# The pool projection as seven products in the mix, and the time step moved into the first gate block

## The chip, the cores and the metric

One core of a Trainium2 chip runs the whole program. The metric is device time in microseconds (us), the median of repeated runs. The engines of the core are named as in the profile: PE multiplies matrices, with PEld loading its stationary operand; DVE works on vectors; ACT evaluates activations and copies; POOL is the general engine, whose queue also issues DMAs; SP only issues DMAs. Each engine executes its own instructions in a fixed order and waits for others by semaphores. PE writes to PSUM, which has eight banks here; everything else is in SBUF or in memory.

## What is computed

One layer of a streaming encoder for 256 prompt tokens and 8 x 16 sample tokens together: T = 384 tokens, model width 2048, all in float32. The parts that matter here:

```
P = rmsnorm(x) @ w_in           # pool 2048 | z 4096 | x,B,C 6144 | dt 64 | two gates 4096
A = pool_mixer(pool part)       # windowed means minus self, a 512x512 map per group, a scale
B = ssd_scan(conv(x,B,C), dt) -> gated norm        # 4096 wide, state-space branch
m = sigmoid(g_A) * (A @ w_pool_proj) + sigmoid(g_B) * (B @ w_ssd_proj)
x = x + rmsnorm(m @ w_out)
x = x + rmsnorm(relu(rmsnorm(x) @ w_up)^2 @ w_down)
```

The change concerns `A @ w_pool_proj` (384 x 2048 by 2048 x 2048), where it is computed, and the small part `dt` (softplus, cumulative sums and their exponentials for 64 heads).

## The kernel before

**Products.** PE multiplies float32 as three products of a high and a low part: every operand x is split into h (a rounded copy, made on ACT) and l = x - h (made on DVE). A 128 x 1024 tile of a weight is one unit: SP loads it (`wfetch`), ACT and DVE split it (`wsplit`, lines 71 and 72, or `split`, 1166 and 1167) into tiles `wh` and `wl` of a ring of three each, and PE uses it in three matmuls per 128 rows of it. A tile of the ring is given out again when its last reader is done. The tile framework sorts the instructions of each engine once, at build time, mainly in program order and by what is ready; `behind(i)` and `later()` put instructions behind one, or behind the last weight split, on the same engine only.

**Direct projections.** `moving` multiplies the activations (stationary) by weight tiles (512 moving columns) for three blocks of 128 tokens: 18 matmuls for a unit, 8 units for an output block of 512 columns when the depth is 2048. `gate` does so for a gate block; after each unit it calls a hook, in which other work is traced. Line 155 to 157 are its three matmuls.

**Seven products.** `quad` multiplies by tile sums in the manner of Strassen and Winograd: a pair of token blocks, two halves of the depth and two halves of the output take 7 products instead of 8, and the third token block rides along with 4, so there are 11 products (of 2 x 3 matmuls, lines 1215 to 1217) for what is 12 directly. A quad covers 512 rows of the weight and 1024 columns of the output (`np_` is the half of the output). Its seven forms, in `ORDER`, each take one weight tile or one sum of weight tiles. Two tiles are added by a DMA of POOL's queue (line 1179), three sums are made on DVE (1202). The nine accumulators m per half are tiles of `acc`; those in `SEEDED` are copied by ACT into PSUM before the products and back after them (1187, 1192), the others are added on DVE (1194). `DIFFS` are five differences of activation tiles that the products need (line 1284, DVE), `refill` splits the activation tiles (ACT, DVE), `aload` fetches them from memory. `converted` turns the accumulators into the product, by seven additions.

**Order of the stages.** (1) The pool input is projected for 16 tiles, windowed and mapped per group; the first gate block `ga0` stands between (`gate_a`). At the end `dt_phase` computes the time step, then the last group is mapped; `pool_map` leaves the 16 pooled tiles in SBUF, split, as A. (2) `pool_out` multiplies A by `w_pp` directly, for four output blocks. The first is multiplied by its gate, the others are stored in memory. `dt_turn` turns the time step over by PE behind the first block. (3) Eight groups of the state-space branch, each with ten projections; at the end two gate blocks of the second gate (`gb0`, `gb1`). Each group stores its tiles in memory (`a_scr`). (4) The mix: the gate blocks `gb2`, `ga1`, `ga2`, `ga3` and part of `gb3` are multiplied unit by unit, and after each unit the hook traces a number of forms of `A_ssd @ w_ssd` (8 groups x 2 quads x 7 = 112 forms over 34 hooks). `gate_late` multiplies a gate by the stored pool product. (5) The merged m is turned over and multiplied by `w_out`. (6) The MLP, whose down projection also runs as quads between the units of the up projection.

Of the kernel before, what the change touches and what calls it, by code (L numbers as in the profile page):

```python
# [6 lines left out]
F32 = mybir.dt.float32  # L7
# [10 lines left out]
NB = 8  # L18
# [8 lines left out]
NWARM = 6  # L27

# [5 lines left out]
def build(ctx, tc, io):  # L34
# [180 lines left out]

    def newton(y, a, hm):
# [14 lines left out]
    def norm_bc(pool, sumsq, n, name, after=None, parts=None):  # L231
# [12 lines left out]
    pp_scr, ma_scr, gb_scr = (  # L244
        [[dram.tile([P, 512], F32, name=f"{nm}_scr{i}_{b}") for b in range(3)] for i in range(4)] for nm in ("pp", "ma", "gb")
    )
    t_scr = [dram.tile([T, P], F32, name=f"t_scr{i}") for i in range(40)]
# [155 lines left out]
    with tc.tile_pool(name="phc", bufs=1, reuse_waits="tile") as pc, tc.tile_pool(name="phc2", bufs=2, reuse_waits="tile") as pc2:  # L403
        pst = pc.tile([P, KD, NB, 15], F32, name="pst")
        gp.dma_start(pst, io["state_pool"])
        bufs = []
        for i in range(2):
# [3 lines left out]
        A = [  # L411
            (pc.tile([P, T], F32R, name=f"ah{n}"), pc.tile([P, T], F32R, name=f"al{n}")) for n in range(KD)
        ]
# [60 lines left out]
        def pool_map(gi, after=None):  # L474
            for hf in range(2):
                h, l = wload(io["pool_w"][gi, hf], f"pw{gi}_{hf}")
                for n2 in range(2):
                    n = gi * 4 + hf * 2 + n2
                    o = sstile(f"pw{n}")[:, :T]
                    with behind(after):  # L480
# [3 lines left out]
                    ah, al = (halves(a) for a in A[n])  # L484
                    sc = vec[:, V_PSC + n : V_PSC + n + 1]
                    s.activation(ah, even_odd(o), AF.Copy, scale=sc)
                    v.scalar_tensor_tensor(
                        out=al, in0=even_odd(o), scalar=sc, in1=ah.bitcast(F32), op0=ALU.mult, op1=ALU.subtract
                    )

        def gate_a(hook):
            sg = [pc.tile([P, 512], F32, tag=f"sg{b}", name=f"sg{b}") for b in range(3)]
            o = three("ga0")

            def done(b):
                with later():
                    sigmoid(sg[b], o, b)

            gate("w_ga", 0, o, done, hook)
            return sg  # L500

        def pool_out(nb, sg):
            o = three(f"pp{nb}")

            def done(b):
                if nb == 0:
                    v.tensor_tensor(sg[b], o[b], sg[b], ALU.mult)
                    gp.dma_start(ma_scr[0][b], sg[b])
                    return
                t = pc.tile([P, 512], F32, tag=f"sg{b}", name=f"po{nb}_{b}")  # L510
                s.copy(t, o[b])
                gp.dma_start(pp_scr[nb][b], t)

            moving(o, units_of("w_pp", nb), A, 1, done)

        def dt_phase(pb):
            ps = mmtile("pj_dt")[:, :T]
            for q in range(2):
# [6 lines left out]
                for k in range(8):  # L525
                    c = hl[:, k].rearrange("p a n -> p (a n)")
                    te.matmul(pairs(ps), c, woven(xg[q * 8 + k][0]), start=q + k == 0, stop=False)
                    te.matmul(pairs(ps), c, woven(xg[q * 8 + k][1]), start=False, stop=q * 8 + k == KD - 1)
# [10 lines left out]
            s.activation(e, ab, AF.Exp, scale=-1.0)  # L539
            v.tensor_scalar(t1, e, 2.0, None, ALU.add)  # L540
# [4 lines left out]
            for i in range(8, 0, -1):  # L545
                v.scalar_tensor_tensor(out=q, in0=q, scalar=1.0 / (2 * i + 1), in1=t2, op0=ALU.add, op1=ALU.mult)
            v.scalar_tensor_tensor(out=q, in0=q, scalar=1.0, in1=t1, op0=ALU.add, op1=ALU.mult)
# [6 lines left out]
            sy.dma_start(cum_scr, cum)  # L554
            nb = n64("nb")
# [21 lines left out]
        def dt_turn(srcs):  # L577
            for r in range(2):
                part = srcs[r * 8 : r * 8 + 8]
                o = sstile(f"tk{r}")  # L580
                for i, a in enumerate(part):
                    te.transpose(o[:, i * NH : i * NH + NH], a, ident[:NH, :NH])
# [10 lines left out]
        for gi in range(4):  # L593
            for k4 in range(4):
# [5 lines left out]
                if gi and k4 == (gi == 1):  # L600
                    if gi == 1:
                        count = []

                        def hook():
                            count.append(1)
                            if waiting and len(count) % 2 == 0:
                                with later():
                                    waiting.pop(0)()
# [1426 lines left out]
```

## Time and profile before

| | |
|---|---|
| median of three runs | 2581.05 us (2579.37 to 2581.16) |
| the profiled execution | 2581.39 us |
| its span, first to last instruction | 2579.6 us |
| pool stage, to the first product of the old pool projection | 0 to 200.3 us |
| old pool projection | 200.3 to 325.9 us |
| state-space groups and two gate blocks | 325.9 us to about 1092 |
| the mix | about 1092 to 1465 us |
| merge and output projection | about 1465 to 1605 us |
| MLP | about 1605 us to the end |

In the rows of the profile, a row of the timeline has start, length, engine, line, operation, the tiles that it writes and reads, shapes, and in brackets the idle time before it and what ended that. A row of a group ends in its busy time, the mean length of one in ns, and its idle time. A row of a stretch has the busy time and count of instructions of PE, PEld, DVE, ACT and POOL, then the granted clock, the DMA share and GB/s. A row of waits has who waited for whom: us in total, times, longest.

### The profile page before, as it was taken

Reading aid. Unit: us, or ns where it says so; the run is one execution under the profiler, and the core shown is the slowest. Engines: PE = TensorE matmul, PEld = TensorE weight load, DVE = VectorE, ACT = ScalarE, POOL = GpSimd, SP = SyncE. Lnnn points to the kernel's source line nnn. Section 1 sums busy time; section 2 is a strip of 40 time slices with the busy share of each in tenths; the row PEclk is TensorE's granted clock in tenths of the full one; section 3 lists DMA queues with packets and bytes.
Section 4 is the critical chain, followed back from the end, with each engine's and each line's share of the span. In section 5 each row is a group of like instructions: output and inputs, shape, how many; then the busy total and the mean of one; then the engine's idle time right before and its main releaser. Section 6 shows DMA issues by size and latency. Waiting matters only on the chain.

```text
span 2579.6 us, 39759 instructions
## 1 busy us (share of the span) xinstructions
PE 2568.2 (100%) x15001; PEld 2397.8 (93%) x15001; DVE 1952.8 (76%) x2745; ACT 1618.9 (63%) x2546; POOL 433.2 (17%) x625
## 2 busy tenths in 40 slices
PE   9999999999999999999999999999999999999998
PEld 9998899999999999888888888999999999999997
DVE  6676367999999998678888855767777776777778
ACT  6443365657566665577888634666766666666665
POOL 0000043455445444110110200000000000000000
PEclk9999999999999999999999999999999999999999
DMA  7444476666766676576676655654555554555554
GB/s 280 148 135 156 158 234 211 232 212 222 246 223 228 219 242 229 197 250 191 204 220 176 204 166 193 207 158 150 155 158 170 162 165 147 156 156 164 160 158 155
DMA packets 141808, 489.82 MB, mean 190 GB/s; under 512 B 21376, under 2 KB 25792, under 8 KB 136368
## 3 DMA queue, kind: packets, MB, share of 16 engines
q1 hardware_dynamic: 100544, 355.93, 41.5%
q0 software_dynamic: 34016, 116.54, 15.9%
q10 hardware_dynamic: 7056, 14.81, 1.8%
q8 instruction: 118, 1.93, 0.3%
q14 instruction: 74, 0.61, 0.1%
HBM read 438.11 MB, written 49.09 MB: 189 GB/s over the span
## 4 chain that ended last, share of the span: by engine, by line
PE 97%; DVE 1%; ACT 1%; issue 0%; DMA 0%; DVEq 0%; ACTq 0%
PE pj_up L102 6%; PE pj_up L104 6%; PE pj_up L103 6%; PE wd L1216 6%; PE wd L1217 6%; PE wd L1215 6%; PE pj_x L102 5%; PE pj_x L103 5%; PE pj_x L104 5%; PE pj_z L103 3%; PE pj_z L102 3%; PE pj_z L104 3%; PE sq L1216 2%; PE sq L1217 2%; PE sq L1215 2%; PE pp L156 2%
## 5 line engine op out<-in xcount | busy, mean ns | idle before, releaser
L102 PE MATMUL pj_up<-x1h,wh_up 128*128 128x384 f32 (+1 forms) x1024 | 333.7, 326 | 0.0
L103 PE MATMUL pj_up<-x1l,wh_up 128*128 128x384 f32 (+1 forms) x1024 | 333.4, 326 | 0.0
L104 PE MATMUL pj_up<-x1h,wl_up 128*128 128x384 f32 (+1 forms) x1024 | 333.4, 326 | 0.0
L71 ACT ACTIVATE wh_up<-w_up 128x1024 fp32r<-128x1024 f32 x126 | 133.2, 1057 | 218.1 <-PE pj_up L103 204.7
L102 PE MATMUL pj_x<-xgh,wh_x 128*128 128x384 f32 x768 | 251.9, 328 | 0.0
L103 PE MATMUL pj_x<-xgl,wh_x 128*128 128x384 f32 x768 | 250.4, 326 | 0.0
L104 PE MATMUL pj_x<-xgh,wl_x 128*128 128x384 f32 x768 | 250.4, 326 | 0.0
L103 PEld LDWEIGHTS pj_up<-x1l,wh_up 128*128 128x128 f32 x1024 | 193.6, 189 | 2.8
L102 PEld LDWEIGHTS pj_up<-x1h,wh_up 128*128 128x128 f32 x1024 | 193.6, 189 | 2.8
L72 DVE TENSOR_TENSOR wl_up<-w_up,wh_up 128x1024 fp32r<-128x1024 f32 x126 | 154.0, 1223 | 53.5 <-ACT wh_up L71 53.5
L104 PEld LDWEIGHTS pj_up<-x1h,wl_up 128*128 128x128 f32 x1024 | 193.6, 189 | 0.0
L102 PE MATMUL pj_z<-xgh,wh_z 128*128 128x384 f32 x512 | 166.9, 326 | 0.0
L103 PE MATMUL pj_z<-xgl,wh_z 128*128 128x384 f32 x512 | 166.9, 326 | 0.0
L104 PE MATMUL pj_z<-xgh,wl_z 128*128 128x384 f32 x512 | 166.9, 326 | 0.0
L1179 POOL DMA_DIRECT2D w_b_wd<-w_down x30 | 25.8, 860 | 831.1 <-DMA w_b_wd<-w_down 348.9
L102 PEld LDWEIGHTS pj_x<-xgh,wh_x 128*128 128x128 f32 x768 | 145.1, 189 | 2.1 <-issue 0.4
L103 PEld LDWEIGHTS pj_x<-xgl,wh_x 128*128 128x128 f32 x768 | 145.2, 189 | 0.0
L104 PEld LDWEIGHTS pj_x<-xgh,wl_x 128*128 128x128 f32 x768 | 145.2, 189 | 0.0
L1192 ACT COPY acc<-wd 128x512 f32<-128x512 f32 x214 | 124.6, 582 | 24.1 <-PE wd L1217 24.0
L71 ACT ACTIVATE wh_x<-w_x 128x1024 fp32r<-128x1024 f32 x96 | 100.4, 1052 | 62.5 <-PE pj_z L103 29.0
L72 DVE TENSOR_TENSOR wl_x<-w_x,wh_x 128x1024 fp32r<-128x1024 f32 x96 | 116.8, 1220 | 27.9 <-ACT wh_x L71 27.9
L1215 PE MATMUL wd<-wh_b_wd,fh 128*128 128x512 f32 x360 | 136.4, 379 | 0.0
(478 smaller groups left out, 7605.2 us busy)
## 6 DMA issues: line engine op xcount, KB each, us to landing
w_up<-w_up SPq DMA_DIRECT2D x128, 512.0 KB, 4.1
w_b_wd<-w_down SPq DMA_DIRECT2D x120, 512.0 KB, 4.3
w_x<-w_in SPq DMA_DIRECT2D x96, 512.0 KB, 4.0
w_z<-w_in SPq DMA_DIRECT2D x64, 512.0 KB, 3.9
w_b_sq<-w_ssd SPq DMA_DIRECT2D x64, 512.0 KB, 4.7
w_ga<-w_ga SPq DMA_DIRECT2D x32, 512.0 KB, 4.2
w_pp<-w_pp SPq DMA_DIRECT2D x32, 512.0 KB, 3.3
hs<-ssm POOLq DMA_DIRECT2D x16, 1024.0 KB, 6.4
```

Of the source, the lines that this page charges most:

```text
L71: cut[0] = s.activation(h, w, AF.Copy)
L72: cut[1] = v.tensor_tensor(l, w, h.bitcast(F32), ALU.subtract)
L102: te.matmul(out, wh, xh, start=first, stop=False, **how)
L103: te.matmul(out, wh, xl, start=False, stop=False, **how)
L104: return te.matmul(out, wl, xh, start=False, stop=last, **how)
L156: te.matmul(out, mh, vl, start=False, stop=False)
L1179: gp.dma_start(w, unit(0, np_ * 2), accum_op=ALU.add)
L1192: s.copy(dst, o)
L1215: te.matmul(out, mh, vh, start=begin, stop=False, skip_group_check=held)
L1216: te.matmul(out, mh, vl, start=False, stop=False, skip_group_check=held)
L1217: te.matmul(out, ml, vh, start=False, stop=end, skip_group_check=held)
```

## The change

The pool projection leaves its stage and becomes the first four of twelve groups of quads in the mix. `pool_map` no longer splits the pooled tiles: it scales them and stores them in memory (`p_scr`), and `aload` fetches them like the others. After its last quad of each half, `branch_a` converts the accumulators and multiplies them by the stored gate (`stage_load`, two extra tiles), and the product is stored in `ma_scr`; then the state-space groups begin anew in the same accumulators. The mix has 168 forms over the same 34 hooks, in steps of about six, two and six. The time step becomes a generator whose parts are traced in the hooks of the first gate block. The first convolution projection stands ahead of the last group's map. Gate blocks are exchanged: `ga1`, `ga2` close the state-space stage, `ga3`, `gb0`, `gb1`, `gb2` are in the mix. The five differences of all groups but the first are computed on POOL, and in the half `np_ = 0` the product m = 3 is no longer seeded. The convolution's state is loaded earlier, and the pooled stage's tiles are moved up by a pad.

```diff
+    def stored(key, nb, o, tiles, hook=None, **span):
+        def done(b):
+            with later():
+                sigmoid(tiles[b], o, b)
+            gp.dma_start((ga_scr if key == "w_ga" else gb_scr)[nb][b], tiles[b])
+
+        gate(key, nb, o, done, hook, **span)
...
-                    ah, al = (halves(a) for a in A[n])
-                    sc = vec[:, V_PSC + n : V_PSC + n + 1]
-                    s.activation(ah, even_odd(o), AF.Copy, scale=sc)
-                    v.scalar_tensor_tensor(
-                        out=al, in0=even_odd(o), scalar=sc, in1=ah.bitcast(F32), op0=ALU.mult, op1=ALU.subtract
-                    )
+                    a = pc2.tile([P, T], F32, tag="po", name=f"po{n}", bufs=3)
+                    s.activation(halves(a), even_odd(o), AF.Copy, scale=vec[:, V_PSC + n : V_PSC + n + 1])
+                    gp.dma_start(p_scr[n], a)
...
         def dt_phase(pb):
             ps = mmtile("pj_dt")[:, :T]
+            w_dt = []
             for q in range(2):
                 w = wpool.tile([P, 1024], F32, tag="w", name=f"w_dt{q}")
                 hl = wpool.tile([P, 8, 2, NH], F32R, tag="wh", name=f"wh_dt{q}")
...
-                for k in range(8):
-                    c = hl[:, k].rearrange("p a n -> p (a n)")
-                    te.matmul(pairs(ps), c, woven(xg[q * 8 + k][0]), start=q + k == 0, stop=False)
-                    te.matmul(pairs(ps), c, woven(xg[q * 8 + k][1]), start=False, stop=q * 8 + k == KD - 1)
+                w_dt.append(hl)
+            yield
+            with behind(last[0]):
+                for k in range(KD):
+                    c = w_dt[k // 8][:, k % 8].rearrange("p a n -> p (a n)")
+                    te.matmul(pairs(ps), c, woven(xg[k][0]), start=k == 0, stop=False)
+                    last[0] = te.matmul(pairs(ps), c, woven(xg[k][1]), start=False, stop=k == KD - 1)
+            yield
...
+        def gate_a():
+            count = []
+
+            def hook():
+                count.append(1)
+                with later():
+                    if waiting and len(count) % 2 == 0:
+                        waiting.pop(0)()
+                    elif len(count) > 2:
+                        next(dt_steps)
+
+            stored("w_ga", 0, three("ga0"), [pc.tile([P, 512], F32, name=f"sg{b}") for b in range(3)], hook)
...
+                if gi == 1 and k4 > 1:
+                    with later():
+                        next(dt_steps, None)
+                if (gi, k4) == (2, 1):
+                    dt_turn()
+        b0 = conv_in(17, 0)
+        pool_map(3, last[0])
...
-    def diffs(gk, which=slice(0, 5)):
+    def diffs(gk):
         x = raw[gk]
-        for o, a, b in DIFFS[which]:
-            v.tensor_tensor(x[:, o], x[:, a], x[:, b], ALU.subtract)
+        for o, a, b in DIFFS:
+            (gp if gk else v).tensor_tensor(x[:, o], x[:, a], x[:, b], ALU.subtract)
...
+    def stage_load(np_):
+        for nb in (np_ * 2, np_ * 2 + 1):
+            stage[nb] = pg0.tile([P, 3, 512], F32, tag=f"e{nb % 2}", name=f"gas{nb}")
+            for b in range(3):
+                gp.dma_start(stage[nb][:, b], ga_scr[nb][b])
+
+    def branch_a(np_):
+        def product(nb, b):
+            g = stage[nb][:, b]
+            v.tensor_tensor(g, hacc(acc, b, nb), g, ALU.mult)
+            gp.dma_start(ma_scr[nb][b], g)
+
+        return converted(lambda m: acc[:, np_ * 9 + m]) + [
+            lambda nb=nb, b=b: product(nb, b) for nb in (np_ * 2, np_ * 2 + 1) for b in range(3)
+        ]
...
+            if gk == 3 and t == 0 or gk == 4 and t == 0:
+                stage_load(gk - 3)
+            if gk == 3 and np_ == 1 or gk == 4 and np_ == 0:
+                if i == 0:
+                    todo.extend(branch_a(gk - 3))
+                with later():
+                    for _ in range(2 if i < 6 else 1):
+                        todo.pop(0)()
...
                 if t == 6:
                     refill(gk + 1, "s2")
-                elif t in (7, 8):
-                    diffs(gk + 1, slice(0, 3) if t == 7 else slice(3, 5))
+                elif t == 7:
+                    diffs(gk + 1)
                 elif t > 10:
                     refill(gk + 1, ("b11", "b21", "U")[t - 11])
...
+            SEEDED if np_ else tuple(m for m in SEEDED if m != 3),
...
+    rates = [6] * 8 + [2] * 7 + [6] * 17
+    while len(WANT) < 34:
+        WANT.append(WANT[-1] + rates[len(WANT) - 2])
+    WANT[2:] = [round(w * 7 * 24 / WANT[-1]) for w in WANT[2:]]
...
-    gate_b(2, mixed("gb2"), gtiles("gbt2"), hooked)
-    for nb in range(1, 4):
-        gate_late(nb, mixed(f"ga{nb}"), hook)
+    stored("w_ga", 3, mixed("ga3"), gtiles("gat3"), hook)
+    for nb in range(3):
+        stored("w_gb", nb, mixed(f"gb{nb}"), gtiles(f"gbt{nb}"), hook)
```

Here t counts the fourteen forms of a group, i the seven of a quad, and `KEYS` names the tiles that each form splits.

## What was predicted

> **What bounds the kernel now.** I read the page first (span, busy shares, clock, chain), then who waits for whom on PE, then PE's instructions in order of time, then the stretches.
>
> ```profile
> span 2579.6 us, 39759 instructions
> PE 2568.2 (100%) x15001; PEld 2397.8 (93%) x15001; DVE 1952.8 (76%) x2745; ACT 1618.9 (63%) x2546; POOL 433.2 (17%) x625
> ...
> PEclk9999999999999999999999999999999999999999
> ...
> PE 97%; DVE 1%; ACT 1%; issue 0%; DMA 0%; DVEq 0%; ACTq 0%
> ```
>
> PE is busy 2568.2 of 2579.6 us at the full granted clock, and 97% of the chain that ended last is PE. So time goes away only with matmuls, and comes back only where PE waits. A busy PE still hides short waits, because matmuls overlap; their rate is read from starts. Two matmuls of the old pool projection, 192 apart with only its own kind between:
>
> ```profile
> 261.75 0.38 PE L155 MATMUL pp<-wh_pp,ah 128*128 128x512 f32 x1
> ...
> 303.19 0.38 PE L155 MATMUL pp<-wh_pp,ah 128*128 128x512 f32 x1
> ```
>
> (303.19 - 261.75) / 192 = 0.2158 us each, not the 0.38 of one record. In the groups of PE by shape the old projection and the seven-product mix have the same record length:
>
> ```profile
> L156 PE MATMUL pp<-wl_pp,ah 128*128 128x512 f32 x192 | 72.9, 380 | 0.0
> L1216 PE MATMUL sq<-wl_b_sq,ahb 128*128 128x512 f32 x160 | 60.9, 380 | 0.5 <-DVE wl_b_sq L1167 0.5
> ```
>
> so I price both at 0.2158. Where PE does wait now, it is in the mix, for splits on DVE:
>
> ```profile
> PE sq L1216 <- DVE wl_b_sq L1167: 0.5, 2, 0.3
> PE gb L156 <- DVE wl_gb L72: 0.4, 1, 0.4
> PE ga L156 <- DVE wl_ga L72: 0.3, 1, 0.3
> ```
>
> and in the stretches (busy us and instruction counts of PE, PEld, DVE, ACT, POOL):
>
> ```profile
> 160.00:180.00 20.00, 20.00 (x125) 20.00 (x124) 15.10 (x31) 9.11 (x16) 0.54 (x1) 1.00 0.38 120
> 180.00:200.00 20.00, 19.94 (x123) 19.51 (x122) 17.26 (x32) 10.65 (x18) 1.08 (x2) 1.00 0.48 151
> ...
> 1160.00:1440.00 280.00, 279.36 (x1292) 243.36 (x1291) 233.78 (x272) 228.51 (x351) 40.85 (x59) 1.00 0.66 201
> 1140.00:1160.00 20.00, 19.79 (x91) 16.91 (x91) 15.73 (x18) 18.54 (x31) 5.80 (x10) 1.00 0.72 224
> 1180.00:1200.00 20.00, 20.00 (x94) 17.51 (x93) 15.78 (x19) 16.91 (x29) 0.88 (x1) 1.00 0.63 183
> 1240.00:1260.00 20.00, 19.71 (x92) 16.95 (x91) 16.71 (x23) 16.48 (x27) 7.21 (x11) 1.00 0.73 253
> 1320.00:1340.00 20.00, 19.72 (x92) 16.81 (x91) 17.36 (x20) 17.96 (x28) 4.75 (x8) 1.00 0.61 189
> ```
>
> A clean 20 us of the mix holds 94 matmuls. Those with 91 or 92 lie where one gate block gives way to the next and ACT has three sigmoids more. Each of the three lost 2 to 3 matmuls, about 0.5 us; the whole mix loses some 2.5 us.
>
> **The change, part by part.**
>
> *Matmuls.* The old projection is 4 output blocks x 8 weight tiles x 18 = 576 matmuls of 512 columns. The new one is 4 groups x 2 halves x 11 products x 6 = 528. So 48 go: 48 x 0.2158 = **-10.4 us**. The time-step matmuls (32) and the convolution projection (48) only move.
>
> *Old pool stage.* Its 32 splits on ACT and DVE lay under PE and are worth nothing. Three waits end with it: 123 matmuls stand in 180 to 200 where the stretch ahead of it has 125, which is 0.3 us at (20 / 125 =) 0.16 each, and one pp matmul came 0.2 late:
>
> ```profile
> 192.26 0.48 ACT raw L534
> 192.76 1.28 ACT L535
> 194.25 0.42 ACT dh L470
> ...
> 204.55 0.44 PE pp L156
> ```
>
> Those are the copy out of the time-step sum, the table load behind it and the last pool split in one ACT queue. In the new order the 48 matmuls of `conv_in(17, 0)` (7.8 us) lie ahead of the last group map and hide that split. **-0.5 us**. The 16 stores of pooled tiles and the earlier load of the convolution state go to POOL's queue, where only later stores wait behind them: nothing.
>
> *Time step in the first gate block.* `dt_phase` splits both time-step weight tiles at the third hook and multiplies at the fifth. Both `wh` tiles come from the ring of three that the gate's units use. Between the hooks, units 3 and 4 share the one slot left. That a split starts only when the matmuls that held its slot are done is seen in the ACT and DVE order of a gate block:
>
> ```profile
> 1082.40 1.06 ACT L71 ACTIVATE wh_gb<-w_gb 128x1024 fp32r<-128x1024 f32 x1 [2.83 <-PE gb L157]
> 1086.29 1.06 ACT L71 ACTIVATE wh_gb<-w_gb 128x1024 fp32r<-128x1024 f32 x1 [2.83 <-PE gb L157]
> ...
> 1087.37 1.23 DVE L72 TENSOR_TENSOR wl_gb<-w_gb,wh_gb 128x1024 fp32r<-128x1024 f32 x1 [1.06 <-ACT wh_gb L71]
> ```
>
> With three slots this costs nothing: the split is used two units later. With one, PE waits for the 1.06 us split on ACT and the 1.23 us one on DVE, less the one matmul (0.22) that needs only the first, plus handovers: 2.2 us. Twice: **+4.4 us**. Bounds: 0, if some slot comes free after all; 6, if DVE work of the time step (its chain is 15 to 20 small operations) lies ahead of the split each time. I take 4.4, which the three rows give. Unit 5 is covered by the time-step matmuls (32 x 0.16 = 5.2 us).
>
> *The mix.* It grows from 112 forms (one of a quad's seven products and its upkeep) to 168, between the same 34 hooks, and the gates that move in or out of it are as many as before. A form is on average 66 / 7 = 9.43 matmuls or 2.03 us, a gate unit 18 or 3.88. Before, a round was 3.61 forms and one unit: 52 matmuls, 11.24 us, 24.9 rounds in the stretch of 280 us. Per round ACT has 228.51 / 24.9 = 9.2 us and DVE 9.4. Taking out the gate's part:
>
> ```profile
> L71 ACT ACTIVATE wh_ga<-w_ga 128x1024 fp32r<-128x1024 f32 x23 | 24.4, 1059 | 2.1 <-PE sq L1217 1.9
> L214 ACT ACTIVATE ga<-ga,yx 128x512 f32<-128x512 f32 x9 | 6.0, 666 | 2.7 <-PE ga L157 2.7
> ...
> L72 DVE TENSOR_TENSOR wl_ga<-w_ga,wh_ga 128x1024 fp32r<-128x1024 f32 x23 | 28.1, 1222 | 3.5 <-ACT wh_ga L71 3.2 <-DMA w_b_sq<-w_ssd 0.3
> L1194 DVE TENSOR_TENSOR acs<-sq,acs 128x512 f32<-128x512 f32 x25 | 17.1, 684 | 0.0
> L1284 DVE TENSOR_TENSOR ax<-ax 128x256 f32<-128x256 f32 x30 | 12.0, 420 | 0.7 <-DMA ax<-a_scr 0.5
> ```
>
> (1.06 and 0.24 of sigmoid on ACT; 1.22 and 0.25 of products on DVE), a form costs ACT 2.19 us and DVE 2.19. After, a round is 6.15 forms and a unit: PE 16.4 us. ACT has 6.15 x 2.19 + 1.3 = 14.8, less 0.5 for the copies that the half no longer seeded for product 3 saves: 14.3 (87%, before 82%). DVE: the five differences per 14 forms go to POOL (5 x 0.42 / 14 = 0.15 per form), the addition in place of a seeded copy comes (0.68 per 14 forms): 6.15 x 2.04 + 1.22 + 0.3 = 14.1 (86%, before 83%). No engine overtakes PE, but what is left to catch up after a gate's end falls from 18% to 13%. I double the 0.5 us at each of its four ends, less what the rarer ends give back: **+1.5 us**, between -2.5 (no waits left) and +10 (below). Loads: each quad's first sum of two weight tiles is made by an adding DMA of POOL's queue, far ahead of its use; here the third such DMA and the third use:
>
> ```profile
> 1121.10 0.87 POOL L1179 DMA_DIRECT2D w_b_sq<-w_ssd  x1 [11.78 <-DMA w_b_sq<-w_ssd]
> ...
> 1150.98 1.05 ACT L1166 ACTIVATE wh_U_sq<-w_b_sq 128x1024 fp32r<-128x1024 f32 x1
> ```
>
> 30 us from issue to use, so POOL work of a few us ahead of it costs nothing. The DMA share in the mix is 0.66, and bytes per us rise little.
>
> *Differences on POOL.* No POOL operation of 256 columns is in the trace. The nearest is the sum of squares over 384:
>
> ```profile
> 544.92 1.01 POOL L952 TENSOR_TENSOR ssum<-ssum,ysq 128x384 f32<-128x384 f32 x1 [4.40 <-ACT ysq L951]
> 548.42 4.00 POOL L952 TENSOR_TENSOR ssum<-ssum,ysq 128x384 f32<-128x384 f32 x1 [0.41 <-ACT ysq L951]
> ...
> 503.69 4.64 POOL L952 TENSOR_TENSOR ssum<-ssum,ysq 128x384 f32<-128x384 f32 x1 [0.34 <-ACT ysq L951]
> ...
> L866 DVE SCALAR_TENSOR_TENSOR xd<-xD,vec,xd x16: 745/1498/1506, 374.3 to 1036.7; 128x512 fp32r<-128x512 f32 x16
> ```
>
> Beside DVE operations that read PSUM it takes 1.01 us; beside back-to-back ones on SBUF it waits, 4.00 to 4.64 in all, and then the DVE operation it got in front of takes 1.50 instead of 0.75. So a difference may hold DVE up by nothing (in a gap) to 1.0; I take 0.75: 5 x 0.75 x 6.15 / 14 = 1.65 per round, DVE 15.7 of 16.4 (96%). Still under PE: **0** in the sum. [...]
>
> **Sum**: -10.4 - 0.5 + 4.4 + 1.5 = -5.0 us on the profiled execution's 2581.4 (its span and 1.8 around it), or 2576.4. The median of the runs is 0.3 lower: **2576.0**.
>
> **Rivals.**
> 1. *The gate block finds its slot*, or ACT and DVE are so early that the wait is small: the 4.4 goes, 2571.5. For it: both engines have room there. Against: two of three slots are plainly held. 0.22.
> 2. *The mix's middle and start go over.* In seven rounds the rate falls to 2 forms, and 26 conversions and products are added: DVE 2 x 2.04 + 1.22 + 0.54 for POOL + 26 x 0.68 / 7 = 8.4 against PE's 36.9 x 0.2158 = 8.0, so 2.6 us in seven rounds. And the first added weight is wanted one unit sooner, where ACT waited for it already:
>
> ```profile
> 1106.73 1.06 ACT L1166 ACTIVATE wh_U_sq<-w_b_sq 128x1024 fp32r<-128x1024 f32 x1 [2.87 <-DMA w_b_sq<-w_ssd]
> ...
> ax<-a_scr POOLq DMA_DIRECT2D x28, 192.0 KB, 5.8
> ```
>
> up to 2.5 us. 2576 + 5 = 2581: no change. 0.22.
> 3. *Slower: the differences starve on POOL.* A group's tile is asked for at its fifth form, issued in about 3 us, landed 5.8 later, so three and a half forms on (2.67 us a form with its share of the gate). If each of the first four differences then waits 4.64 us, as the longest row does, the fourth ends 18.6 us later, one us after the next group's second key needs it; the ACT copy that reads it holds up the splits behind it. With 0.5 of handover this is 1.5 us in each of 11 groups: 2576 + 16 = 2592. It decides where DVE leaves no gap for some 4.4 us at a time. Against: a DVE that waits for ACT leaves gaps, and additions out of PSUM (25 in 280 us) leave POOL alone. 0.15.
>
> That the 48 matmuls don't go away is excluded by the code.
>
> **How the numbers follow.** The forecast has 0.41. A measurement tells about 0.2% (5.2 us: below 2575.9, above 2586.2). The forecast stands at that edge: half of it is faster (0.21), half the same (0.20). Faster: 0.21 + 0.22 = 0.43; slower: rival 3 and a little of 2, 0.17; same: 0.40. The range 2570 to 2590 reaches past the first rival and leaves out the upper part of the third.
>
> **What would show it.** PE should have 48 matmuls fewer, all 512 wide. In the first gate block PE should wait twice for a split, some 2 us each, or, by rival 1, not at all. In the mix DVE's busy share should stay under 97%, with waits at the ends of gate blocks; POOL's differences should take 0.7 to 4.6 us each; and no ACT copy of a difference should wait for POOL, or rival 3 is at work. I am wrong if PE waits anywhere else by over 2 us.

## The result

The changed kernel takes 2609.64 us (median of 4 runs, 2606.37 to 2610.54) against 2581.11 (2579.37 to 2583.16) for the kernel before on the same chip: ratio 1.0108, 95% interval 1.009 to 1.0125. It is slower by 28.5 us, or 1.1%. The forecast was 2576.0 us, with a range from 2570 to 2590.

The page of the changed kernel (span; busy time, share and instructions of each engine; shares of the chain that ended last):

```profile
span 2608.7 us, 40054 instructions
PE 2573.3 (99%) x14953; PEld 2388.7 (92%) x14953; DVE 2035.8 (78%) x2810; ACT 1688.4 (65%) x2675; POOL 531.7 (20%) x730
...
PE 88%; DVE 4%; issue 3%; DMA 2%; ACT 2%; POOL 0%; SPq 0%; DVEq 0%; ACTq 0%; POOLq 0%
```

The 48 matmuls are gone (15001 to 14953), and the chain that was 97% PE is 88% PE: other engines and loads now end waits. The same view of who waits for whom on PE (total us, times, longest):

```profile
PE sq L1205 <- ACT wh_b_sq L1156: 8.9, 5, 3.8
PE sq L1206 <- DVE wl_b_sq L1157: 5.2, 8, 1.2
PE gb L157 <- DVE wl_gb L73: 3.5, 6, 0.8
PE ga L156 <- ACT wh_ga L72: 2.8, 3, 1.2
PE ga L157 <- DVE wl_ga L73: 1.6, 4, 0.6
```

Before, the longest such wait behind the warm-up was 0.4. The stretches (PE's matmuls in the first bracket, its granted clock third from last, then DMA share and GB/s):

```profile
980.00:1000.00 20.00, 14.77 (x53) 10.98 (x51) 13.52 (x20) 11.36 (x18) 7.84 (x11) 0.83 1.03 355
1180.00:1200.00 20.00, 16.81 (x69) 13.85 (x68) 13.30 (x12) 11.96 (x18) 6.67 (x7) 0.91 0.61 197
1300.00:1320.00 20.00, 17.32 (x72) 14.32 (x71) 14.82 (x15) 12.97 (x20) 6.91 (x6) 0.91 0.55 168
1420.00:1440.00 20.00, 18.30 (x82) 15.15 (x82) 16.75 (x16) 15.81 (x25) 8.97 (x9) 1.00 0.65 193
```

A clean 20 us of the mix holds 94 matmuls; these hold 53, 69, 72 and 82. A finer measure is used from here on, "lost time": for every matmul the step from its start to the next start, less the median step of its kind, summed over steps more than 15 ns too long. It gives

| lost us | before | after |
|---|---|---|
| start of the program (0 to 25) | 1.0 | 3.0 |
| first gate block (55 to 85) | 0.0 | 4.1 |
| mix (1088 to 1512; 970 to 1490) | 3.6 | 37.5 |
| whole program | 48.3 | 88.6 |

The last row is 40.2 us more; less the 10.4 of the matmuls that leaves 29.8, and the spans are 29.1 apart. Of these 40.2 us, 33.9 lie in the mix. Its 37.5 us are 10.2 in its first 40 us, some 15 at five places (1122, 1181, 1301, 1343 and 1423 us), and the other 12 in many waits under 1.3 us.

**One of the five places.** ACT's instructions ahead of the gap at 1181, POOL's queue, then PE:

```profile
1174.17 1.06 ACT L1156 ACTIVATE wh_X_sq<-w_b_sq 128x1024 fp32r<-128x1024 f32 x1
1182.42 0.42 ACT L1282 ACTIVATE ahs<-ax 128x256 fp32r<-128x256 f32 x1 [7.19 <-DMA ax<-a_scr]
1182.74 1.04 ACT L1156 ACTIVATE wh_b_sq<-w_b_sq 128x1024 fp32r<-128x1024 f32 x1
```

```profile
1168.92 0.75 POOL L1267 DMA_DIRECT2D ax<-a_scr  x1 [3.59 <-issue]
...
1172.89 2.25 POOL L1267 DMA_DIRECT2D ax<-a_scr  x3
```

```profile
1183.83 0.48 PE L1205 MATMUL sq<-wh_b_sq,ahb 128*128 128x512 f32 x1 [2.41 <-ACT wh_b_sq L1156]
1185.09 0.48 PE L1206 MATMUL sq<-wl_b_sq,ahb 128*128 128x512 f32 x1 [0.78 <-DVE wl_b_sq L1157]
...
1186.69 0.63 PE L1206 MATMUL sq<-wl_b_sq,ahs 128*128 128x512 f32 x1
1187.12 0.63 PE L1207 MATMUL sq<-wh_b_sq,als 128*128 128x512 f32 x1
```

ACT had nothing to wait for but the next group's tile: the copy of slot `s2` (`refill` at form 6) reads `ax`, whose four loads were issued at form 4; the last three of them stand behind six stores that lie between these two rows of POOL's queue. Over the whole run, in the view of the tile `ax` (minimum, median, maximum; the first row is of POOL's differences, in ns):

```profile
L1275 POOL TENSOR_TENSOR ax<-ax x55: 716/1329/1764, 998.6 to 1428.8; 128x256 f32<-128x256 f32 x55
...
DMA to landing us min/median/max: 2.9/5.9/10.1
```

The split of the next weight stands behind that copy in ACT's queue, and PE behind the split. The table of waits puts this under "ACT wh_b_sq"; the load shows only in ACT's own rows. Behind the gap matmuls start 0.43 us apart (1187.12 - 1186.69) and not 0.2158, for 3.4 us (eight steps); the granted clock was 0.50 from 1187 to 1189, and the 0.91 for the 20 us from 1180 fits that (3.4 us at 0.50 take off 0.085).

**The start of the mix**, on ACT:

```profile
981.93 0.63 ACT L1282 ACTIVATE ahb<-ax 128x512 fp32r<-128x512 f32 x1 [2.23 <-DMA ax<-p_scr]
...
984.79 1.06 ACT L1156 ACTIVATE wh_b_sq<-w_b_sq 128x1024 fp32r<-128x1024 f32 x1 [0.42 <-DMA w_b_sq<-w_pp]
...
992.20 1.06 ACT L1156 ACTIVATE wh_U_sq<-w_b_sq 128x1024 fp32r<-128x1024 f32 x1 [4.70 <-DMA w_b_sq<-w_pp]
```

ACT waits for loads there (DMA share 1.03), and PE behind ACT: it stands from 982 to 986 for the first tiles.

**The start of the program.** On POOL, and ACT's second copy of the input after and before:

```profile
1.38 0.68 POOL L450 DMA_DIRECT2D cstate<-state_conv  x1 [0.33 <-issue]
```

```profile
8.78 0.61 ACT L322 ACTIVATE xgh<-xw,x0g 128x384 fp32r<-128x384 f32 x1 [4.25 <-DMA xw<-xw]
```

```profile
6.36 0.62 ACT L312 ACTIVATE xgh<-xw,x0g 128x384 fp32r<-128x384 f32 x1 [1.81 <-DMA xw<-xw]
```

The load of the convolution state (648 KB) now runs beside the first input tiles, which land 2.4 us later. In the kernel before it was issued at 327.5 us.

### The profile page after: what moved, and what is told of

Read it like the earlier page. It is cut to its first block, busy times and chain, and to the rows that moved or that the text cites. A ratio compares the mean times of both kernels' runs of the same rounds, so it can differ in the third digit from the quotient of the medians.

```text
span 2608.7 us, 40054 instructions
## 1 busy us (share of the span) xinstructions
PE 2573.3 (99%) x14953; PEld 2388.7 (92%) x14953; DVE 2035.8 (78%) x2810; ACT 1688.4 (65%) x2675; POOL 531.7 (20%) x730
## 4 chain that ended last, share of the span: by engine, by line
PE 88%; DVE 4%; issue 3%; DMA 2%; ACT 2%; POOL 0%; SPq 0%; DVEq 0%; ACTq 0%; POOLq 0%
PE pj_up L103 6%; PE pj_up L105 6%; PE pj_up L104 6%; PE wd L1207 5%; PE wd L1206 5%; PE wd L1205 5%; PE pj_x L103 5%; PE pj_x L105 5%; PE pj_x L104 5%; PE pj_z L105 3%; PE pj_z L104 3%; PE pj_z L103 3%; PE sq L1206 2%; PE sq L1207 2%; PE sq L1205 2%
## 5 line engine op out<-in xcount | busy, mean ns | idle before, releaser
L103 PE MATMUL pj_up<-x1h,wh_up 128*128 128x384 f32 x768 | 250.5, 326 | 0.0
L104 PE MATMUL pj_up<-x1l,wh_up 128*128 128x384 f32 x768 | 250.4, 326 | 0.0
L105 PE MATMUL pj_up<-x1h,wl_up 128*128 128x384 f32 x768 | 250.4, 326 | 0.0
L103 PEld LDWEIGHTS pj_up<-x1h,wh_up 128*128 128x128 f32 x768 | 145.2, 189 | 1.2
L104 PEld LDWEIGHTS pj_up<-x1l,wh_up 128*128 128x128 f32 x768 | 145.2, 189 | 1.2
L105 PEld LDWEIGHTS pj_up<-x1h,wl_up 128*128 128x128 f32 x768 | 145.2, 189 | 0.0
L1206 PE MATMUL wd<-wl_b_wd,fh 128*128 128x512 f32 x360 | 136.4, 379 | 0.0
```

Of the source, the lines that this page charges most:

```text
L103: te.matmul(out, wh, xh, start=first, stop=False, **how)
L104: te.matmul(out, wh, xl, start=False, stop=False, **how)
L105: return te.matmul(out, wl, xh, start=False, stop=last, **how)
L1206: te.matmul(out, mh, vl, start=False, stop=False, skip_group_check=held)
```

## The experiments

All are edits of the changed kernel. Medians; the ratio to the kernel before, timed beside it on the same chip, with its interval; lost time in the mix. The short names are those that the expectations use. The runs of the letters e, f, g, h and i were taken on five chips, where the kernel before took 2580.2 to 2581.6 us, so between letters the ratios compare better than the medians.

| run | us | ratio | lost in the mix |
|---|---|---|---|
| changed kernel | 2609.6 | 1.0108 (1.009 to 1.0125) | 37.5 |
| e1, s2 later | 2602.3 | 1.0081 (1.0066 to 1.0096) | 29.3 |
| e2, mix later | 2600.8 | 1.0077 (1.0062 to 1.0092) | 27.3 |
| e3, time-step tiles of its own | 2608.3 | 1.0100 (1.0084 to 1.0117) | 38.1 |
| e4, differences on DVE | 2608.7 | 1.0105 (1.009 to 1.012) | 38.0 |
| f1, convolution state later | 2605.7 | 1.0093 (1.0078 to 1.0108) | 31.5 |
| f2, mix later, gate tiles later | 2602.5 | 1.0084 (1.0069 to 1.0099) | 27.9 |
| f3, all five, differences on POOL | 2591.9 | 1.0044 (1.0028 to 1.0061) | 22.8 |
| f4, all five, differences on DVE | 2591.9 | 1.0043 (1.0028 to 1.0057) | 23.6 |
| g1, f3 with the unit behind b21 | 2585.1 | 1.0013 (1.0004 to 1.0023) | 16.3 |
| g2, f3 with the unit behind W | 2599.3 | 1.0071 (1.0056 to 1.0086) | 29.8 |
| g3, f3 with flat rates | 2596.8 | 1.0063 (1.0046 to 1.0079) | 26.5 |
| g4, f3 with all seeded | 2595.9 | 1.0059 (1.0044 to 1.0074) | 26.1 |
| h1, g1 with s2 ahead of the unit | 2585.5 | 1.0016 (1.0007 to 1.0025) | 17.0 |
| h2, h1 with differences on DVE ahead of it | 2582.3 | 1.0004 (0.9995 to 1.0013) | 13.7 |
| h3, h2 with own load of the time step | 2581.9 | 1.0002 (0.9993 to 1.0011) | 14.4 |
| i1, h3 with refills at 8, 11, 12 | 2582.3 | 1.0003 (0.9995 to 1.0012) | 13.4 |
| i2, h3 with refills at 8, 10, 11 | 2580.8 | 0.9996 (0.9987 to 1.0005) | 12.8 |

**1. The copy that waits for the load.**

```diff
-                if t == 6:
+                if t == 9:
                     refill(gk + 1, "s2")
```

> Changed kernel with one edit: the copy and the difference of slot s2 of the next group (ACT and DVE) are issued at form 9 of the group and not at form 6; the load of the group stays at form 4, the differences stay at form 7 on POOL. Theory A (the load, issued at form 4, lands after ACT has reached the copy at form 6, and the splits behind it in ACT's queue make TensorE wait): the waits of ACT L1282 for the load of ax (7.2, 3.7, 2.5, 2.3, 1.8, 1.1 us in the changed kernel) go, and with them the TensorE gaps at about 1122, 1181, 1301, 1343 and 1423 us, some 13 to 15 us in all: 2609.6 - 14 = 2595 to 2597. Theory B (DVE is too full, because POOL's differences hold it up and the mix is denser): the copy's place doesn't matter, 2607 to 2610, and the gaps turn up elsewhere.

7.4 us less, about half of theory A's gain. ACT's waits for `ax` past the first group are gone, and so are PE's gaps at 1181 and 1301, but the one at 1424 stayed (1.5 us lost), and a new gap of 2.1 us came at 1192. On POOL and DVE there, and on PE:

```profile
1185.66 7.61 POOL L1275 TENSOR_TENSOR ax<-ax 128x256 f32<-128x256 f32 x5 [4.09 <-DMA ax<-a_scr]
...
1187.60 5.09 DVE L1192 TENSOR_TENSOR w_b_sq<-w_b_sq,w_b_sq 128x1024 f32<-128x1024 f32 x3
1192.61 1.74 DVE L1157 TENSOR_TENSOR wl_b_sq<-w_b_sq,wh_b_sq 128x1024 fp32r<-128x1024 f32 x1
```

```profile
1194.41 0.48 PE L1206 MATMUL sq<-wl_b_sq,ahb 128*128 128x512 f32 x1 [1.97 <-DVE wl_b_sq L1157]
...
1195.17 0.63 PE L1206 MATMUL sq<-wl_b_sq,ahb 128*128 128x512 f32 x1
1195.59 0.63 PE L1207 MATMUL sq<-wh_b_sq,alb 128*128 128x512 f32 x1
```

Three additions at 1.7 us and a split at 1.74, not 1.22, beside POOL's differences: theory A holds for the gaps that went, and theory B for the one that came.

**2. The mix one gate unit later.**

```diff
-    WANT = [0, 0]
+    WANT = [0, 0, 0]
...
-        if done_[0] == 1:
+        if done_[0] == 2:
             diffs(0)
...
-        elif done_[0] == 2:
+        elif done_[0] == 3:
```

> Changed kernel with one edit: the differences and copies of group 0 and the first forms come one gate unit later (hooks 2, 3 and 4 as in the kernel before, not 1, 2 and 3), the same forms spread over one hook less. Theory A (the mix starts before its first tiles and weights have landed: TensorE stands from 981.7 to 985.9, and waits again for the first added weight): the stretch 980 to 1000 loses some 10 us more than its matmuls need; a unit of 3.9 us ahead of it covers the first gap, part of the wait for the added weight and the slowed clock behind the gap: 2609.6 - 6 to - 9 = 2601 to 2604. Theory B (the start costs nothing that the unit can cover; the mix is short of DVE): 2608 to 2611.

8.8 us less, which is the size that theory A gave, but mostly not for its reason: of the 10.2 us lost in the first 40 us of the mix 7.3 remain, so only 2.9 of the gain lie where theory A put it. The other 7.3 of the 10.2 us that the mix lost less lie further on: the gaps at 1181 and 1301 went, others of 1.2 to 1.4 came, and ACT's waits for `ax` from `a_scr` fell from 18.6 to 9.9 us. The likely reason is that the groups now meet the units elsewhere; experiments 7 to 9 test the place of the units by itself.

**3. The ring in the gate block** (the pad gives up the room).

```diff
-                hl = wpool.tile([P, 8, 2, NH], F32R, tag="wh", name=f"wh_dt{q}")
+                hl = pb.tile([P, 8, 2, NH], F32R, name=f"wh_dt{q}")
```

> Changed kernel with one edit: the two split time-step weights have tiles of their own and take no slot of the ring of three that the gate's units use. If the ring is what TensorE waits for in the first gate block (1.31 + 0.51 and 1.36 + 0.51 us beside the step of its neighbours), these 3.7 us go and nothing else changes: 2605 to 2607. If the place of the split in ACT's and DVE's queue is the cause, the gaps stay: 2609 to 2611.

PE's waits in the gate block, changed kernel, then this run:

```profile
68.54 0.92 PE L156 MATMUL ga<-wh_ga,xgh 128*128 128x512 f32 x3 [1.15 <-ACT wh_ga L72]
69.80 0.48 PE L157 MATMUL ga<-wl_ga,xgh 128*128 128x512 f32 x1 [0.34 <-DVE wl_ga L73]
...
74.50 0.91 PE L156 MATMUL ga<-wh_ga,xgh 128*128 128x512 f32 x3 [1.20 <-ACT wh_ga L72]
```

```profile
68.92 0.91 PE L156 MATMUL ga<-wh_ga,xgh 128*128 128x512 f32 x3 [0.21 <-ACT wh_ga L72]
70.44 0.48 PE L157 MATMUL ga<-wl_ga,xgh 128*128 128x512 f32 x1 [0.61 <-DVE wl_ga L73]
```

The second wait is gone, the first shorter: lost time there falls from 4.1 to 1.4 us. The ring was the cause of these 2.7 us. The medians are only 1.3 apart, inside their intervals, as start and mix lost more in some runs.

**4. The differences back on DVE.**

```diff
-            (gp if gk else v).tensor_tensor(x[:, o], x[:, a], x[:, b], ALU.subtract)
+            v.tensor_tensor(x[:, o], x[:, a], x[:, b], ALU.subtract)
```

> Changed kernel with one edit: the five differences of each group go back to DVE, all five at form 7. Theory A (loads are late): they stand on DVE and wait there for the whole load of the group, which lands 1.5 to 2 us after what the copy waits for, so DVE is held up too: no gain, 2609 to 2617. Theory B (POOL's differences hold up DVE, whose splits run 1.7 us beside them instead of 1.2, 5 in each of 11 groups): the hold-up of some 0.5 us per difference goes, 2609.6 - 10 to - 25 = 2585 to 2600.

No change, as theory A has it: while the loads come late, it does not matter which engine makes the differences.

**5. The load of the convolution state behind that of the pooling state.**

```diff
-        gp.dma_start(pst, io["state_pool"])
-        gp.dma_start(cst_, io["state_conv"])
+        with behind(gp.dma_start(pst, io["state_pool"])):
+            gp.dma_start(cst_, io["state_conv"])
```

> Changed kernel with one edit: the load of the convolution state (648 KB) is queued on POOL behind that of the pooling state, which waits for memory until about 27 us; in the changed kernel it is issued 1.4 us after the start. Theory A (it takes bandwidth from the first input tiles, which ACT and DVE then wait for): the stretch 0 to 20 lost 2.3 to 6.1 us beside its matmuls in the five traced runs with the early load, 1.0 before; it goes back to about 1.0, 2609.6 - 2 to - 4 = 2605 to 2608, and the times of the runs lie closer together (4 us apart so far, 2 us for the kernel before). Theory B (the starts differ by chance): nothing changes, 2608 to 2611.

4.0 us less, at the edge of the intervals. The traces are clearer: lost time at the start was 3.0, 4.9, 3.7, 2.2, 6.1 and 5.0 us in the six traced kernels with the early load (mean 4.2), and 0.9 to 2.8 (mean 1.6) in the twelve with the later one. So the early load cost about 2.6 us on average; in this pair alone the start lost only 0.7 less (2.3 against 3.0), and the rest of what the trace of this run saves is in the mix (31.5 against 37.5), where the edit changes nothing. The times of the runs stayed as far apart (2602.0 to 2607.0), so that part of the expectation failed.

**6. The stored gate tiles loaded later**, on top of the mix one unit later; `loaded[0]` is the last load of the group before.

```diff
-                stage_load(gk - 3)
+                with behind(loaded[0]):
+                    stage_load(gk - 3)
```

> The kernel with the mix one gate unit later, with one more edit: the loads of the stored gate tiles for groups 3 and 4 (gas, L1293, 256 KB each, 6 of them at once) are queued on POOL behind the load of the group before, so that they no longer run at the start of the mix, where the DMA share is 1.03 and every load lands 8 to 18 us after its issue. Theory A (the start of the mix is bound by DMA): 1.5 of some 9 MB less in this stretch; the first weight sum lands earlier by up to 4 us and the waits of 1.9, 1.0 and 2.3 us left there and the slow clock behind them shrink: 2600.8 - 2 to - 5 = 2596 to 2599. Theory B (the order of ACT and DVE, not the loads, sets it): 2600 to 2602.

Theory A was wrong: 1.6 us more than without it, which is inside the intervals. The 1.5 MB are not what the first weight sum waits for.

**All five together** (1, 2, 3, 5, 6), with the differences on POOL, and on DVE with three at form 8 and two at form 10:

> All five edits together (slot s2 at form 9, mix one unit later, time step with tiles of its own, convolution state later, stored gate tiles later), differences still on POOL. If the causes are separate, their gains add: 2609.6 - 7.4 - 8.8 - 2 - 3 - 3 = about 2585, 2581 to 2589. If POOL's differences hold up DVE now that they run in full beside its splits, it stays over 2588.

> The same five edits, and the differences on DVE, three at form 8 and two at form 10. Theory A (POOL's differences cost DVE some 0.5 us each where splits are wanted, which is what is left in the mix): 3 to 7 us under the run with the differences on POOL, 2577 to 2582. Theory B (they cost nothing that counts): within 2 us of that run, or above it, as DVE has 0.42 x 55 = 23 us more work.

2591.9 both times: the gains do not add up in full (that would be 2585), and the engine of the differences again makes no difference. Lost time at the start is 0.9 and 1.7, in the gate block 1.4 and 1.7. In the mix 23 us are left, 6 to 7 of them in its first 40 us; every wait of PE that the profile lists there is for a split.

**7 to 9. Where the gate's units lie in the quads.** On top of all five, the list of forms between hooks (31 numbers, sum 168) behind `b21` of every quad, behind `W`, and even:

```diff
-    rates = [6] * 8 + [2] * 7 + [6] * 16
+    rates = [2] + [7] * 7 + [2] * 6 + [1] * 2 + [7] * 14 + [5]   # behind b21
+    rates = [5] + [7] * 6 + [2] * 6 + [1] * 2 + [7] * 15 + [2]   # behind W
```

> The kernel with the five edits (f3, 2591.9) and another list of forms between the gate's units: 2, then 7 at a time (2 or 1 in the middle), so that a unit lies behind b21 of every quad, just ahead of U, b22 and W, and the first unit comes after two forms. Theory A (DVE falls behind in the run of U, b22 and W, whose splits and additions take DVE 3 x 2.3 = 6.9 us while TensorE needs 24 matmuls or 5.2 us, so a unit of 3.9 us with one split ahead of this run is worth most there): the waits for DVE splits in the mix (some 11 us) fall by half or more and so does the wait of 2.8 us for the first weight sum, 2591.9 - 5 to - 9 = 2583 to 2587. Theory B (what counts is only the mean load of DVE): 2590 to 2593.

> The same, with the unit behind W of every quad (5 forms first, then 7 at a time), so that U, b22 and W follow b11 and b21 without a unit ahead of them. Theory A: as much as f3 or worse, 2591 to 2600, and over 4 us above the run with the unit behind b21. Theory B: equal to that run within 2 us.

> The five edits, and the forms spread evenly, 5 or 6 after each unit, with no thinner middle. Theory A (place of the units in the quad): the units drift through the quads as in f3, and the middle with its 26 conversions and products has more forms: 2592 to 2598. Theory C (6 instead of 5.4 forms per unit is what makes the mix late outside the middle): 2586 to 2591.

2585.1, 2599.3 and 2596.8: each is in the range of theory A, and the same work is 14.2 us apart by the list alone. Not all of this is the place in the quad: behind `b21` the list also begins with two forms and not five, and the first 40 us of the mix lost 3.4 us against 6.4. From 1010 us on, 13.0 and 23.4 us were lost, so the unit's place within the quad is worth some 10. PE's waits behind b21, then behind W:

```profile
PE sq L1206 <- DVE wl_b_sq L1157: 6.4, 11, 1.8
...
PE gb L157 <- DVE wl_gb L73: 0.4, 1, 0.4
```

```profile
PE gb L157 <- DVE wl_gb L73: 7.4, 11, 0.8
PE sq L1206 <- DVE wl_b_sq L1157: 4.9, 4, 2.1
```

With the unit behind W, DVE comes out of the run late and PE waits for the unit's own split, 11 times some 0.7 us. DVE's queue through the run of U, b22 and W, from h3 (experiment 12), where nothing disturbs it:

```profile
1254.20 1.22 DVE L1157 TENSOR_TENSOR wl_U_sq<-w_b_sq,wh_U_sq 128x1024 fp32r<-128x1024 f32 x1
1255.33 0.68 DVE L1184 TENSOR_TENSOR acs<-sq,acs 128x512 f32<-128x512 f32 x1
1255.93 1.21 DVE L1192 TENSOR_TENSOR w_b_sq<-w_b_sq,w_b_sq 128x1024 f32<-128x1024 f32 x1
1257.07 1.22 DVE L1157 TENSOR_TENSOR wl_b_sq<-w_b_sq,wh_b_sq 128x1024 fp32r<-128x1024 f32 x1
1258.20 2.35 DVE L1192 TENSOR_TENSOR w_b_sq<-w_b_sq,w_b_sq 128x1024 f32<-128x1024 f32 x2
1260.47 1.22 DVE L1157 TENSOR_TENSOR wl_W_sq<-w_b_sq,wh_W_sq 128x1024 fp32r<-128x1024 f32 x1
```

From 1254.20 to 1261.69 DVE works without a gap for 24 matmuls, 24 x 0.2158 = 5.2 us of PE. A unit just ahead (3.9 us of PE, one split of 1.22 on DVE) gives DVE the 2.3 us that it lacks.

**10. Product 3 seeded in both halves again**, on top of all five.

```diff
-            SEEDED if np_ else tuple(m for m in SEEDED if m != 3),
+            SEEDED,
```

> The five edits, and product 3 of the first half starts from a copy on ACT again instead of an addition on DVE at its end (0.68 us of DVE less and 0.5 us of ACT more in 14 forms, 11 times). Theory A or B (TensorE waits for DVE): 1 to 3 us less than f3, 2589 to 2591. If ACT is as late as DVE: no change or a little more, 2591 to 2594.

The expectation was wrong: 4.0 us more, with intervals that overlap, and 3.3 more lost in the mix. Between 1010 and 1460 us DVE waited for ACT 57.2 us in all, against 45.3 in f3, so the copies that ACT got back made it late in its turn: ACT is no freer than DVE here.

**11. s2, and the differences, just ahead of the unit**, on top of the unit behind b21; in h1 the differences stay at form 7 on POOL, in h2 they are on DVE:

```diff
-            (gp if gk else v).tensor_tensor(x[:, o], x[:, a], x[:, b], ALU.subtract)   # h2 only
+            v.tensor_tensor(x[:, o], x[:, a], x[:, b], ALU.subtract)                   # h2 only
...
-                if t == 9:
+                if t == 8:
                     refill(gk + 1, "s2")
-                elif t == 7:                 # h2 only
                     diffs(gk + 1)
```

> The kernel with the unit behind b21 (g1, 2585.1) with the copy and difference of slot s2 at form 8, just ahead of the unit, and not at form 9 behind it; differences on POOL. Theory A (what lies between U and W on DVE makes TensorE wait): the als difference (0.4 to 0.95 us) goes out of this run, 2585.1 - 1 to - 3. Theory B (only the sum counts): 2584 to 2587.

> The same, and the five differences on DVE at form 8, just ahead of the unit, none on POOL. Theory A with POOL as the cause of what is left (DVE's splits and additions run 1.75 us beside POOL's differences instead of 1.22, some 5 of them in each of 11 groups just in the run of U, b22 and W): 2 to 5 us less than with POOL's differences, 2578 to 2583. If POOL's differences cost nothing in sum, as in the pair f3 and f4: no change or 1 to 2 us more, since DVE has 5 x 0.42 us more in each group.

The place of s2 gave nothing. The differences on DVE gave 3.2 us, timed side by side, with intervals that overlap a little. The split of U on DVE by shape in the mix, and the differences, on POOL and then on DVE (busy us, mean ns):

```profile
L1157 DVE TENSOR_TENSOR wl_U_sq<-w_b_sq,wh_U_sq 128x1024 fp32r<-128x1024 f32 x24 | 33.5, 1396 | 6.7 <-ACT wh_U_sq L1156 6.7
...
L1276 POOL TENSOR_TENSOR ax<-ax 128x256 f32<-128x256 f32 x55 | 75.0, 1392 | 54.0 <-DMA ax<-a_scr 39.1 <-DMA ax<-p_scr 14.9
```

```profile
L1157 DVE TENSOR_TENSOR wl_U_sq<-w_b_sq,wh_U_sq 128x1024 fp32r<-128x1024 f32 x24 | 29.2, 1218 | 4.2 <-ACT wh_U_sq L1156 4.2
...
L1276 DVE TENSOR_TENSOR ax<-ax 128x256 f32<-128x256 f32 x60 | 21.1, 417 | 1.8 <-DMA ax<-p_scr 1.8
```

On POOL they run right in the run of U, b22 and W and stretch DVE's work there; on DVE they lie ahead of the unit, where there is room. The edit changes the engine and the place of the differences together, and no run has them on POOL at another place, so which of the two gave the 3.2 us is not shown.

**12. The rest: the loaded tile in the gate block (h3), and the refills at a group's end (i1, i2).**

```diff
-                w = wpool.tile([P, 1024], F32, tag="w", name=f"w_dt{q}")
+                w = pb.tile([P, 512], F32, name=f"w_dt{q}")
...
                     refill(gk + 1, "s2")
+                    refill(gk + 1, "b11")
...
-                elif t > 10:
-                    refill(gk + 1, ("b11", "b21", "U")[t - 11])
+                elif t in {11: 'b21', 12: 'U'}:
+                    refill(gk + 1, {11: 'b21', 12: 'U'}[t])
```

The first edit is h3; the others, on top of it, are i1, and i2 has 10 and 11 in place of 11 and 12.

> The same as the run with the differences on DVE ahead of the unit, and the unsplit time-step weights also have tiles of their own, so that they take no slot of the ring of loaded weights. In the first gate block ACT waited 2.9 us for the load of a gate unit behind them, and TensorE 1.2 + 0.5 us for its split. If the slot of the loaded tile is what was late: 1.3 to 1.9 us less than that run, 2576 to 2581. If not: equal to it.

> The last kernel (h3, 2581.9) with the copies of the next group's b11, b21 and U at forms 8, 11 and 12 and not 11, 12 and 13. In h3 the wait left in every group is at its first form: ACT has three of these copies (1.5 us) among the seeding copies of V, X and b11, DVE waits 0.3 us for ACT each time and TensorE 0.6 to 1.0 us for DVE, 9 times. If the place of these copies is the cause: half of these 7 us or more go, 2576 to 2579. If ACT's sum over the whole second half is (it has no gap to move them into): 2580 to 2583.

> The same with b21 and U at forms 10 and 11, so further ahead of the group's end, but in the run of U, b22 and W where DVE is short. By theory A their DVE halves (0.6 and 0.4 us) make TensorE wait there for what they save at the end: 2578 to 2583, above the other run by 1 to 3 us; if DVE has room there by now: equal to it or less, 2574 to 2578.

The loaded tile was not the cause: the gate block still loses 1.3 us, and why stays open. In i1 (2582.3) nothing was gained, so the place of the refills alone was not the cause that its expectation named. i2 is 1.5 us below i1 on the same chip, and not above it as theory A had it: there the waits for `wl_b_sq` of DVE are 1.6 us in all, against 4.7 in h3, while smaller waits came elsewhere. 2580.8 is the best version, equal to the kernel before. PE's waits in h3, then in i2:

```profile
PE sq L1206 <- DVE wl_b_sq L1157: 4.7, 9, 1.0
```

```profile
PE sq L1206 <- DVE wl_b_sq L1157: 1.6, 1, 1.6
...
PE gb L157 <- DVE wl_gb L73: 0.8, 1, 0.8
PE sq L1205 <- ACT wh_V_sq L1156: 0.7, 1, 0.7
```

i2 loses 12.8 us in the mix, 9.2 more than the kernel before, and that with the gate block eats the 10.4 us of the matmuls. What would bring these out, and which of ACT and DVE is short there, stays open.

## Why the prediction was wrong

The terms add up: by matmul counts and lost time, -10.4 (matmuls) - 0.4 (old pool stage) + 4.1 (gate block) + 2.0 (start of the program) + 33.9 (mix) = 29.2 us, and the spans are 29.1 apart. The sum of the prediction was -5.0; almost all of the miss is its term for the mix.

- **Matmuls, -10.4, right.** 48 fewer at the same step of 0.216 us.
- **Old pool stage, -0.5, right**: its late matmuls (0.43 us lost before at 180 to 200) are gone.
- **Time step in the gate block, +4.4, right.** Lost time there is 4.1, in two waits where it was said (1.3 + 0.5 us and 1.4 + 0.5), and they shrink to 1.4 with tiles of its own. The first rival falls with it.
- **The load of the convolution state, "nothing", wrong.** The step looked at what stands behind it on POOL's queue. What it cost lies in the DMAs beside it, and it now runs in the first microseconds: about 2.6 us by the traces.
- **The mix, "No engine overtakes PE ... +1.5 us", wrong, and the failed step of this forecast**: 33.9 us more lost. The step compared the mean load of a round with PE's time, ACT's 87% and DVE's 86%. No mean overtook PE: from 1020 to 1440 us DVE was busy 355.5 and ACT 331.8 of the 420 us. The sign that it named came all the same, waits of PE of up to 3.8 us for a split. Three things lie below the mean. First, six forms come in one burst without a gate unit, so that from form 4 (load) to form 6 (copy) PE needs only 2 x 2.03 = 4.1 us, against 5.9 in the median and up to 10.1 for each load to land; the third rival had both numbers but asked about the differences at form 7 and not about the copy ahead of them. That was some 15 us, slow clock included, of which one edit brings 7.4. Second, the mix begins one unit sooner and with six forms at once, while its first tiles and weights are still being loaded. The second rival saw the place and priced it at 2.5; it is 10.2 against 0.7. One unit later brought 2.9 of that back; how much of the rest is the loads and how much the order of ACT and DVE is not shown. Third, in the run of U, b22 and W DVE is short in each quad, whatever its mean, and where the unit falls is worth some 10 us.
- **Differences on POOL, 0 in the sum, right for the change as made** (no gain by moving them back in experiment 4 and in the pair of all five), for a reason that the prediction did not have: other waits seem to cover them. Once most of these are gone, moving them to DVE and ahead of the unit gains 3.2 us. The third rival, starvation on POOL, did not come: they took 0.72 to 1.76 us, not 4.64, and no copy on ACT waited for POOL. Nor did all of DVE's additions take longer beside them: in the changed kernel those to the accumulators that read PSUM took 0.68 us beside POOL's differences and 0.68 without.

## What to carry to other kernels

A mean share under 100% says little where work comes in bursts: compare supply and demand over the shortest run that has to be fed (here three forms, 7.5 us of DVE for 5.2 of PE), and put the work that relieves the feeding engine just ahead of it (here worth some 10 us). For every instruction that reads a loaded tile, count the time from issue to landing (here 5.9 us in the median, up to 10.1) in instructions of the new, denser order, and look at what stands behind it in its engine's queue. A load that moves can cost the loads it now runs beside, even when no one waits for it (here about 2.6 us at the start).

## What the runs showed of the hardware

**Behind some waits the granted clock was 0.50.** Behind three of the gaps in the changed kernel's mix (at 982, 1181 and 1302 us) matmuls started 0.427 us apart, and not 0.216: seven or eight of them, 1.5 to 1.7 us lost each time. The granted clock was 0.50 there (985 to 991, 1187 to 1189 and 1306 to 1309 us). Behind the gaps whose longest step lost 1.0 to 1.5 us (at 1123, 1344 and 1424) there were none, and the granted clock stayed 1.00. In the run of experiment 1 matmuls started 0.42 us apart behind a single wait in which 2.1 us were lost (rows above). In the run of all five on POOL a longer one lost 2.8 us, the matmuls behind it started 0.21 us apart, and the granted clock was 1.00 in both stretches of 10 us from 990 to 1010:

```profile
993.40 0.48 PE L1206 MATMUL sq<-wl_b_sq,ahb 128*128 128x512 f32 x1 [2.62 <-DVE wl_b_sq L1157]
993.72 0.38 PE L1207 MATMUL sq<-wh_b_sq,alb 128*128 128x512 f32 x1
993.93 0.38 PE L1205 MATMUL sq<-wh_b_sq,ahb 128*128 128x512 f32 x1
```

So the length of the wait alone does not tell the two apart here; what does is not shown.

**POOL against DVE.** In the changed kernel the 55 differences of 128 x 256 on POOL took 0.72 to 1.76 us each, and 0.72 to 0.73 where no DVE instruction ran beside them. DVE's splits and its sums of weight tiles, which read two tiles in SBUF, took about 1.7 us beside them (in the run of experiment 1 5.09 for three, 1.74 for one) where they take 1.22 without: both engines lost time, DVE some 0.5 us an instruction. DVE's additions that read PSUM lost none (0.68 us either way).
